# Attention scores for two heads at once: a contraction of 64 on each row half of TensorE, in place of one head with a contraction of 128

## The chip, the cores and the metric

The kernel runs on one core of a Trainium2 chip. The metric is device time of one execution in microseconds; the kernel before was run three times. One execution was recorded by the hardware profiler, and all rows below come from that recording. The engines are named as in the profile: PE is TensorE (PEld its weight loads), DVE is VectorE, ACT is ScalarE, POOL is GpSimd, SP is SyncE.

## What is computed

Two layers over 1024 latent tokens (a grid of 16 rows and 64 columns) and 256 context tokens, 1024 channels, all in float32. The first layer mixes with Fourier and Hyena channels, the second with neighbourhood attention; each ends in a SwiGLU feed-forward part. The change touches the second layer's attention alone, 16 heads of 64 channels:

```python
s_loc = jnp.einsum("bcqhd,bicjhd->bhcqij", q_r, k_b).astype(jnp.float32) * scale + bias[None]
s_loc = jnp.where(col_ok[:, :, None, :], s_loc, -jnp.inf)
s_ctx = jnp.einsum("bcqhd,bjhd->bhcqj", q_r, kc).astype(jnp.float32) * scale
s = jnp.concatenate([s_loc.reshape(B_, H, n_chunk, NA_QCOLS, n_loc), s_ctx], axis=-1)
p = jax.nn.softmax(s, axis=-1).astype(v.dtype)
```

A query sees the keys of a window around it, with a position bias, and all context keys. The softmax over both is then multiplied with the local and the context values.

## The kernel before

The kernel is written as Python code that records instructions. A scheduler then places them engine by engine, by its own estimate of when each is ready and when a buffer is free. The order in which TensorE does its work is therefore not the order of the code, and it is shown further down.

Most products are split to keep float32's accuracy: a number is written as a high and a low part, and three products are added (high by high, high by low, low by high).

Attention (`attention`, L1990) walks over eight pairs of heads. For each pair, `attn_prep` (L1895) projects keys and queries (`lin`, into the two PSUM banks of the pool `pq`) and loads and splits the values. It runs ahead of the items and is mixed in between their stages, so that its wide f16 products fill TensorE. After the last pair, the first part of the output projection (`first_part`, L2352) takes its place as filler.

The scores are made by `attn_item` (L2016). There are 64 items. Before the change an item is one head, one half of the grid's rows (`hf`) and two of the four column chunks (`c0`, `c0 + 1`), 128 queries in each chunk. A head has only 64 channels, so the code fills the array's 128 rows with the parts of the split: `kk[hd]` holds the keys' high part in the head's own 64 partitions and the low part in the other 64 (L1950 to L1959). The queries' high part must then stand in both halves, and so must the low part. Each of them is first made in its own half (L1971, L1972) and then copied to the other half by a DMA on POOL's queue (L1973 and L1974). Two products, high and low queries against the stacked keys, give all terms; they include low by low.

An item runs in three stages, and three items overlap. First it issues two loads of the bias (POOL's queue) and the scores: for the context, two chunks of 256 columns side by side in one PSUM bank, and for the local keys two banks of 384 columns (12 rows of 32). The matmuls are recorded at the helper's line, L283; 128x256 and 128x384 in f32 identify them. Then come the smallest negated score (DVE, L2041 and L2044), the exponentials (ACT, L2046 and L2048) and the transposes. For 52 of the 64 items the context part goes through a cast (ACT, L2053), a subtraction (POOL, L2054) and a transposing DMA (SP, L2055); the rest is transposed on TensorE (L2062) and split by ACT and DVE (L2065, L2066). The third stage multiplies with the values (128x65 and 128x64, f16), divides (DVE, L2088, L2089) and, after the last item of a row half, turns and stores the result (`attn_out`, L2095). During attention the PSUM tiles of all items take turns in the six banks of the pool `pp`. Before the change an item asks for three banks for scores, two or three for transposes and one for its result.

Of the kernel before, what the change touches and what calls it, by code (L numbers as in the profile page):

```python
# [19 lines left out]
P = 128  # L20
# [181 lines left out]
class Builder:  # L202
# [1692 lines left out]
    def attn_prep(self, pr, u):  # L1895
# [5 lines left out]
        kk = [self.S4(F32R), self.S4(F32R)]  # L1901
# [40 lines left out]
        for pc in (0, 1, 2):  # L1942
            for i, s in enumerate(lin(*wk, pc, acc)):
                if i == 3:
                    value(len(vt))
                if pc == 1 and i == 6:
                    wq = self.halves_of("wq", pr)
                yield s
            w = WID[pc]
            for hd in (0, 1):  # L1950
                own, other = slice(hd * 64, hd * 64 + 64), slice(64 - hd * 64, 128 - hd * 64)
                dst = kk[hd][:, pc * 512:pc * 512 + w] if pc < 2 else kc[:, hd * 256:hd * 256 + 256]
                if pc < 2:
                    nc.scalar.copy(dst[own], acc[pc][own, :w])
                    nc.vector.tensor_tensor(dst[other], acc[pc][own, :w], dst[own].bitcast(F32), SUB)
                else:
                    nc.scalar.mul(dst[own], acc[pc][own, :w], -1.0)
                    nc.vector.scalar_tensor_tensor(dst[other], acc[pc][own, :w], -1.0, dst[own].bitcast(F32),
                                                   op0=MUL, op1=SUB)  # L1959
        nxt = None  # L1960
        for pc in (0, 1):
            for i, s in enumerate(lin(*wq, pc, acc, by_chunk)):
                if i == 3:
                    value(len(vt))
                if pc == 1 and i == 3 and pr < 7:
                    nxt = self.halves_of("wk", pr + 1)
                yield s
            for hd in (0, 1):
                own, other = slice(hd * 64, hd * 64 + 64), slice(64 - hd * 64, 128 - hd * 64)
                qh, ql = self.S2(F32R), self.S2(F32R)  # L1970
                nc.scalar.mul(qh[own], acc[pc][own], self.qinv[own])  # L1971
                nc.vector.scalar_tensor_tensor(ql[own], acc[pc][own], self.qinv[own], qh[own].bitcast(F32), op0=MUL, op1=SUB)  # L1972
                for t in (qh, ql):  # L1973
                    self.ldr(t[other].bitcast(F32), t[own].bitcast(F32))  # L1974
                qs[(hd, pc)] = (qh, ql)
        self.aw = nxt
        self.prep[pr] = (qs, kk, kc, vt)
        yield 0.1

    def attn_load(self, pr):  # L1980

        qs, kk, kc, vt = self.prep[pr]
        for hf in (0, 1):
            osb = {}
            for hd in (0, 1):
                for c0 in (0, 2):
                    yield self.attn_item(pr * 2 + hd, hd, hf, c0, qs[(hd, hf)], kk[hd], kc[:, hd * 256:hd * 256 + 256], vt,
                                         osb, pr if hd == 1 and c0 == 2 else None)
# [27 lines left out]
    def attn_item(self, head, hd, hf, c0, qs, kk, kc, vt, osb, out):  # L2016

        nc, a = self.nc, self.a
        rlo = 4 * hf
        bias, loc = [], []  # L2020
        pctx = self.PS()
        for i in (0, 1):
            c = c0 + i
            b = self.G(F32, 384)
            self.ldr(b, a["bias"][head, hf, c])
# [4 lines left out]
        for i in (0, 1):  # L2030
            c = c0 + i
            q = [t[:, c * P:(c + 1) * P] for t in qs]
            ps = self.PS()
            for part in (0, 1):
                kv = kk.rearrange("p (r w) -> p r w", w=64)[:, rlo:rlo + 12, KSTART[c]:KSTART[c] + 32]
                self.mm(ps[:, :384], q[part], kv, part == 0, part == 1)
            loc.append(ps)
# [3 lines left out]
        nc.vector.tensor_reduce(cm, pctx.rearrange("p (i k) -> p i k", i=2), axis=AX, op=MIN)  # L2041
        pc = self.T()
        for i in (0, 1):
            nc.vector.tensor_tensor_reduce(bias[i], loc[i][:, :384], bias[i], -1.0, cm[:, i:i + 1], ADD, MIN,  # L2044
                                           mx[:, i:i + 1])
            nc.scalar.activation(pc[:, i * 256:i * 256 + 256], pctx[:, i * 256:i * 256 + 256], AF.Exp,  # L2046
# [3 lines left out]
        turned = 8 * (head // 2) + 4 * hf + 2 * hd + c0 // 2 < 52  # L2050
# [21 lines left out]
        for i in (0, 1):  # L2072
            c = c0 + i
            ops = []
            for g in range(3):
                gg = hf + g
                ops.append((pts[1 + i], g, c, 2 * gg + hd))
            for j in range(2):
                ops.append((pts[0], 2 * i + j, 4, 2 * j + hd))
            oo = o[:, i * 65:(i + 1) * 65]  # L2080
            for n, (t, j, cv, k) in enumerate(ops):
# [7 lines left out]
        nc.vector.tensor_tensor(osb[hf][:, c0 * P:c0 * P + 256].rearrange("p (i q) -> p i q", i=2)[:, :, hd * 64:hd * 64 + 64],  # L2089
                                both[:, :, :64], rv.unsqueeze(2).to_broadcast([P, 2, 64]), MUL)  # L2090
        if out is not None:
            self.attn_out(out, hf, osb[hf])
# [419 lines left out]
```

## Time and profile before

| | us |
|---|---|
| median of 3 runs | 2919.67 |
| lowest and highest run | 2909.61, 2922.42 |
| span of the profiled execution, first to last instruction | 2918.2 |
| attention, first scores to last values (from the span's start) | 1808 to 2230 |

The span is one execution and lies 1.5 us under the median of the runs. In a timeline row the columns are start (us from the span's start), length (us), engine, line, operation, output and inputs by tile name, shape and count. After a matmul's "128*128" (rows and columns of the array in use) stands what streams through it, partitions by columns. In a row of groups, after the count, stand busy us and mean ns of one, then the engine's idle time ahead of them and what ended it. In a row of one line, three numbers after the count are the shortest, median and longest duration in ns.

### The profile page before, as it was taken

How to read it: one execution, taken by the hardware profiler on the slowest of the kernel's cores; microseconds unless marked ns; L12 is line 12 of the kernel's file. 1: busy time of each engine (PE TensorE's matmuls, PEld its weight loads, DVE VectorE, ACT ScalarE, POOL GpSimd, SP SyncE). 2: the span in 40 equal slices, each digit the busy share in tenths (PEclk: the TensorE clock that was granted, in tenths of full speed). 3: DMA queues.
4: the chain of work that ended last, by engine and by line, in shares of the span. 5: the costliest groups of instructions: out<-in, count | busy, mean ns of one | idle time of the engine just before them, and what ended most of it. 6: DMA issues, size and time to landing. Idle time of an engine off the chain costs nothing. (4 is left out here: it accounts for less than half of the span.)

```text
span 2918.2 us, 46050 instructions
## 1 busy us (share of the span) xinstructions
PE 2766.6 (95%) x16163; PEld 1714.2 (59%) x16163; DVE 2094.0 (72%) x3833; ACT 1647.7 (56%) x2899; POOL 642.6 (22%) x1057
## 2 busy tenths in 40 slices
PE   6989999999989999999999999999999999999998
PEld 3766557888879644444555844676665444444554
DVE  4778867585467798877886767776676778775765
ACT  4674324454675667654555555676664477654553
POOL 1012013354220121213120012444443022112000
PEclk8989999999999999999999999999999999999999
DMA  6574434358785555566994798777775666424753
GB/s 254 187 265 161 161 122 151 111 168 286 285 344 182 207 205 197 201 213 240 327 333 161 273 337 294 179 188 172 185 198 188 236 226 231 153 93 184 242 191 113
DMA packets 325156, 615.98 MB, mean 211 GB/s; under 512 B 90934, under 2 KB 130552, under 8 KB 324922
## 3 DMA queue, kind: packets, MB, share of 16 engines
q1 hardware_dynamic: 252378, 384.38, 39.9%
q0 software_dynamic: 70240, 224.45, 21.6%
q10 hardware_dynamic: 2304, 4.20, 0.4%
q8 instruction: 127, 2.08, 0.3%
q14 instruction: 107, 0.88, 0.1%
HBM read 455.33 MB, written 135.53 MB: 202 GB/s over the span
## 5 line engine op out<-in xcount | busy, mean ns | idle before, releaser
L1449 PE MATMUL ps<-s,s 128*128 128x512 f16 x2592 | 582.2, 382 | 14.4 <-ACT tk L1454 6.8
L1449 PEld LDWEIGHTS <-s 128*128 128x128 f16 x2640 | 259.0, 98 | 332.6 <-issue 27.8
L283 PE MATMUL ps<-s,wh 128*128 128x256 f32 (+3 forms) x1752 | 398.2, 331 | 11.1 <-ACT wh L287 5.4
L1218 ACT ACTIVATE s<-s,c 128x512 f16<-128x512 f32 (+1 forms) x324 | 233.5, 754 | 141.9 <-DMA s<-d 79.9
L1219 DVE SCALAR_TENSOR_TENSOR s<-s,c,s 128x512 f16<-128x512 f32 (+1 forms) x324 | 247.4, 794 | 84.5 <-ACT s L1218 84.1
L1666 PE MATMUL ps<-s 128*128 128x512 f16 (+2 forms) x1308 | 303.4, 378 | 2.0 <-DVE s L1219 2.0
L283 PE MATMUL pq<-s,wh 128*128 128x512 f16 (+1 forms) x1000 | 280.3, 354 | 9.8 <-DMA wh<-d 5.4
L283 PE MATMUL ps<-s,wl 128*128 128x256 f32 (+3 forms) x876 | 261.6, 331 | 1.3 <-DVE wl L289 1.2
L283 PEld LDWEIGHTS <-wh 128*128 128x128 f16 x1664 | 160.9, 99 | 170.2 <-issue 20.9
L1666 PEld LDWEIGHTS <-s 128*128 128x128 f16 x1536 | 148.5, 98 | 178.9 <-issue 6.5
L274 POOL DMA_DIRECT2D d<-s x201 | 109.0, 543 | 640.5 <-DVE s L1510 178.6
L283 PE MATMUL ps<-s,s 128*128 128x65 f16 (+5 forms) x2666 | 222.3, 236 | 27.5 <-DMA s<-s 11.4
L335 ACT CAST mat<-cs 128x1024 fp32r<-128x1024 f16 (+2 forms) x120 | 111.6, 935 | 140.6 <-PE ps L283 57.3
L283 PEld LDWEIGHTS ps<-s,wh 128*128 128x128 f32 x1088 | 177.5, 192 | 18.1 <-ACT wh L287 5.7
L283 PE MATMUL ps<-s,mat 128*128 128x512 f32 x696 | 184.7, 413 | 3.3 <-DVE s L289 2.9
L1449 PE MATMUL ps<-s,wh 128*128 128x512 f16 x616 | 184.9, 379 | 1.8 <-DVE g L1463 1.4
L283 PE MATMUL pq<-s,wl 128*128 128x512 f16 (+1 forms) x500 | 174.5, 354 | 0.5 <-DMA wl<-d 0.5
L283 PEld LDWEIGHTS <-s 128*128 128x128 f16 x2400 | 114.5, 98 | 82.9 <-DMA s<-s 11.5
L283 PEld LDWEIGHTS ps<-s,mat 128*128 128x128 f32 x696 | 136.5, 199 | 37.9 <-DVE s L289 3.8
L1251 ACT ACTIVATE t<-s 128x1024 bf16<-128x1024 f32 (+1 forms) x164 | 141.9, 867 | 12.2 <-DVE c L470 8.4
L283 PEld LDWEIGHTS ps<-s,s 128*128 128x128 f32 (+1 forms) x746 | 113.6, 192 | 32.1 <-ACT s L287 7.0
L283 PEld LDWEIGHTS <-wl 128*128 128x128 f16 x832 | 82.3, 99 | 77.4 <-issue 4.5
(431 smaller groups left out, 5477.3 us busy)
## 6 DMA issues: line engine op xcount, KB each, us to landing
s<-d SPq DMA_DIRECT2D x294, 256.0 KB, 4.0
d<-s POOLq DMA_DIRECT2D x157, 256.0 KB, 3.2
s<-in_down SPq DMA_DIRECT2D x154, 256.0 KB, 5.4
s<-in_ada_w POOLq DMA_DIRECT2D x48, 512.0 KB, 4.8
g<-in_bias POOLq DMA_DIRECT2D x128, 192.0 KB, 3.6
s<-in_gate SPq DMA_DIRECT2D x46, 512.0 KB, 3.7
s<-in_up SPq DMA_DIRECT2D x46, 512.0 KB, 4.0
d<-g POOLq DMA_DIRECT2D x87, 256.0 KB, 2.9
```

Of the source, the lines that this page charges most:

```text
L274: self.last_ldr = self.nc.gpsimd.dma_start(out, in_).ins
L283: self.nc.tensor.matmul(o, l, r, start=st, stop=sp)
L335: self.nc.scalar.copy(m, st)
L1218: nc.scalar.activation(hi, src, AF.Copy, scale=scale)
L1219: nc.vector.scalar_tensor_tensor(lo, src, scale, hi, op0=MUL, op1=SUB)
L1251: self.nc.scalar.activation(junk[:, :t.shape[1]], t, AF.Abs, scale=2.0 ** -15, accum_out=st[:, k:k + 1])
L1449: nc.tensor.matmul(ps, x[:, sl], y, start=first and j == 0 and x is wh and y is xh, stop=j == 3 and x is wl, skip_group_check=True)
L1666: m = nc.tensor.matmul(acc[j][:, c0:c1], x[:, sl], y[:, xs], start=first and k == 0, stop=last and k == 2, skip_group_check=True)
```

## The change

An item is now one pair of heads with one column chunk; there are still 64 items with two score blocks each. The keys are kept as a high and a low tile that hold both heads, 64 partitions each (`kh`, `kl`), and so are the queries and the negated context keys. The scores of a head are three products with a contraction of 64: high by high, high by low, low by high. The code writes the two heads in turn, head 0 on partitions 0 to 63 and head 1 on 64 to 127, each into a bank of its own, so an item takes four banks for scores in place of three. The copies of the preparation work on 128 partitions at once and are half as many; the DMAs that duplicated the queries are gone. The minimum over the context scores is taken from two banks by two instructions. Transposes, values and output are the same work, indexed by head in place of chunk.

```diff
-        kk = [self.S4(F32R), self.S4(F32R)]
+        kh, kl = self.S4(F32R), self.S4(F32R)
...
-            for hd in (0, 1):
-                own, other = slice(hd * 64, hd * 64 + 64), slice(64 - hd * 64, 128 - hd * 64)
-                dst = kk[hd][:, pc * 512:pc * 512 + w] if pc < 2 else kc[:, hd * 256:hd * 256 + 256]
-                if pc < 2:
-                    nc.scalar.copy(dst[own], acc[pc][own, :w])
-                    nc.vector.tensor_tensor(dst[other], acc[pc][own, :w], dst[own].bitcast(F32), SUB)
...
+            if pc < 2:
+                self.split(acc[pc], *(t[:, pc * 512:pc * 512 + w] for t in (kh, kl)))
+            else:
+                nc.scalar.mul(kc[:, :w], acc[pc][:, :w], -1.0)
+                nc.vector.scalar_tensor_tensor(kc[:, w:], acc[pc][:, :w], -1.0, kc[:, :w].bitcast(F32),
+                                               op0=MUL, op1=SUB)
...
-            for hd in (0, 1):
-                own, other = slice(hd * 64, hd * 64 + 64), slice(64 - hd * 64, 128 - hd * 64)
-                qh, ql = self.S2(F32R), self.S2(F32R)
-                nc.scalar.mul(qh[own], acc[pc][own], self.qinv[own])
-                nc.vector.scalar_tensor_tensor(ql[own], acc[pc][own], self.qinv[own], qh[own].bitcast(F32), op0=MUL, op1=SUB)
-                for t in (qh, ql):
-                    self.ldr(t[other].bitcast(F32), t[own].bitcast(F32))
-                qs[(hd, pc)] = (qh, ql)
+            qh, ql = self.S2(F32R), self.S2(F32R)
+            nc.scalar.mul(qh, acc[pc], self.qinv)
+            nc.vector.scalar_tensor_tensor(ql, acc[pc], self.qinv, qh.bitcast(F32), op0=MUL, op1=SUB)
+            qs[pc] = (qh, ql)
...
-        pctx = self.PS()
-        for i in (0, 1):
-            c = c0 + i
...
-            q = [t[:, c * P:(c + 1) * P] for t in qs]
-            for part in (0, 1):
-                self.mm(pctx[:, i * 256:i * 256 + 256], q[part], kc, part == 0, part == 1)
...
+        pctx, loc = ([self.PS(), self.PS()] for _ in range(2))
+        qc = [t[:, c * P:(c + 1) * P] for t in qs]
+        kw = [t.rearrange("p (r w) -> p r w", w=64)[:, 4 * hf:4 * hf + 12, KSTART[c]:KSTART[c] + 32] for t in kk]
+        for acc, keys, w in ((pctx, kc, 256), (loc, kw, 384)):
+            for x, y in ((0, 0), (0, 1), (1, 0)):
+                for hd in (0, 1):
+                    r = slice(hd * 64, hd * 64 + 64)
+                    self.mm(acc[hd][:, :w], qc[x][r], keys[y][r], x == 0 and y == 0, x == 1)
...
-        nc.vector.tensor_reduce(cm, pctx.rearrange("p (i k) -> p i k", i=2), axis=AX, op=MIN)
...
+            nc.vector.tensor_reduce(cm[:, i:i + 1], pctx[i][:, :256], axis=AX, op=MIN)
```

The scheduler's order shows what becomes of this on TensorE. The first piece is one item of the kernel before, between two stretches of other work. In the first tile after MATMUL (`ps`) the product is gathered, after the arrow stand the two operands, and the size is that of the result; f32 products load their weights themselves and have no row for it:

```order
L283 MATMUL ps_20520<-s_4222_19882,s_4309_20376 128x65
L283 MATMUL ps_20569<-s_4100_19192,s_4205_19818 128x256
L283 MATMUL ps_20569<-s_4100_19192,s_4206_19819 128x256
L283 MATMUL ps_20569<-s_4100_19192,s_4205_19818 128x256
L283 MATMUL ps_20569<-s_4100_19192,s_4206_19819 128x256
L283 MATMUL ps_20578<-s_4099_19191,s_4205_19818 128x384
L283 MATMUL ps_20578<-s_4099_19191,s_4206_19819 128x384
L283 MATMUL ps_20581<-s_4099_19191,s_4205_19818 128x384
L283 MATMUL ps_20581<-s_4099_19191,s_4206_19819 128x384
L2062 MATMUL ps_20601<-c_86,g_20464 128x128 x3
```

Four context products go into one bank and two local products into each of two. The same place of the next item but one in the changed kernel, TensorE again, where the heads alternate throughout (head 0 in 20640 and 20642, head 1 in 20641 and 20643):

```order
L283 MATMUL ps_20640<-s_4102_19209,s_4211_19859 128x256
L283 MATMUL ps_20641<-s_4102_19209,s_4211_19859 128x256
L283 MATMUL ps_20640<-s_4102_19209,s_4211_19859 128x256
L283 MATMUL ps_20641<-s_4102_19209,s_4211_19859 128x256
L283 MATMUL ps_20640<-s_4102_19209,s_4212_19860 128x256
L283 MATMUL ps_20641<-s_4102_19209,s_4212_19860 128x256
L283 MATMUL ps_20642<-s_4100_19207,s_4211_19859 128x384
L283 MATMUL ps_20643<-s_4100_19207,s_4211_19859 128x384
L283 MATMUL ps_20642<-s_4101_19208,s_4211_19859 128x384
L283 MATMUL ps_20643<-s_4101_19208,s_4211_19859 128x384
L283 MATMUL ps_20642<-s_4100_19207,s_4212_19860 128x384
L283 MATMUL ps_20643<-s_4100_19207,s_4212_19860 128x384
```

Twelve products stand where eight stood, in four banks. In the item ahead of it the scheduler has written the three local products of head 0 and then those of head 1, followed by a transpose (L2082 and L2046 are the new lines of L2099 and L2062):

```order
L283 MATMUL ps_20532<-s_4100_19207,s_4211_19859 128x384
L283 MATMUL ps_20532<-s_4101_19208,s_4211_19859 128x384
L283 MATMUL ps_20532<-s_4100_19207,s_4212_19860 128x384
L283 MATMUL ps_20533<-s_4100_19207,s_4211_19859 128x384
L283 MATMUL ps_20533<-s_4101_19208,s_4211_19859 128x384
L283 MATMUL ps_20533<-s_4100_19207,s_4212_19860 128x384
L2082 MATMUL ps_20508<-c_86,s_4273_20153 128x128
```

Here only the third and fourth rows are neighbours on different row halves. In the whole order of the changed kernel the 768 score products stand in 90 unbroken stretches (512 in 94 before). Taken from the front of each stretch, 290 pairs of neighbours on different halves can be formed, and 188 products are left over. 53 of the 90 stretches are followed by transposes and the other 37 by f16 products.

More of the change, by code (lines that the diff above doesn't have):

```diff
@@ L1949, in attn_prep @@
             w = WID[pc]
-            for hd in (0, 1):
-                own, other = slice(hd * 64, hd * 64 + 64), slice(64 - hd * 64, 128 - hd * 64)
-                dst = kk[hd][:, pc * 512:pc * 512 + w] if pc < 2 else kc[:, hd * 256:hd * 256 + 256]
-                if pc < 2:
-                    nc.scalar.copy(dst[own], acc[pc][own, :w])
-                    nc.vector.tensor_tensor(dst[other], acc[pc][own, :w], dst[own].bitcast(F32), SUB)
[L1956 to L1959, printed above, removed]
+            if pc < 2:
[4 more added lines that the diff above has]
+                                               op0=MUL, op1=SUB)
         nxt = None
@@ L1984, in attn_load @@
             osb = {}
[L1985 to L1988, printed above, removed]
+            for c in range(4):
+                yield self.attn_item(pr, hf, c, qs[hf], kk, kc, vt, osb)
     def attention(self, u, fill):
@@ L2014, in attention, with attn_item @@
             pass
-    def attn_item(self, head, hd, hf, c0, qs, kk, kc, vt, osb, out):
+    def attn_item(self, pr, hf, c, qs, kk, kc, vt, osb):
         nc, a = self.nc, self.a
-        rlo = 4 * hf
-        bias, loc = [], []
-        pctx = self.PS()
-        for i in (0, 1):
-            c = c0 + i
+        bias = []
+        for hd in (0, 1):
             b = self.G(F32, 384)
-            self.ldr(b, a["bias"][head, hf, c])
+            self.ldr(b, a["bias"][pr * 2 + hd, hf, c])
             bias.append(b)
-            q = [t[:, c * P:(c + 1) * P] for t in qs]
-            for part in (0, 1):
-                self.mm(pctx[:, i * 256:i * 256 + 256], q[part], kc, part == 0, part == 1)
[L2030 to L2037, printed above, removed]
+        pctx, loc = ([self.PS(), self.PS()] for _ in range(2))
[3 more added lines that the diff above has]
+            for x, y in ((0, 0), (0, 1), (1, 0)):
+                for hd in (0, 1):
+                    r = slice(hd * 64, hd * 64 + 64)
+                    self.mm(acc[hd][:, :w], qc[x][r], keys[y][r], x == 0 and y == 0, x == 1)
         yield
@@ L2040, in attn_item @@
         cm, mx, rv = (st[:, 2 * i:2 * i + 2] for i in range(3))
-        nc.vector.tensor_reduce(cm, pctx.rearrange("p (i k) -> p i k", i=2), axis=AX, op=MIN)
         pc = self.T()
         for i in (0, 1):
+            nc.vector.tensor_reduce(cm[:, i:i + 1], pctx[i][:, :256], axis=AX, op=MIN)
             nc.vector.tensor_tensor_reduce(bias[i], loc[i][:, :384], bias[i], -1.0, cm[:, i:i + 1], ADD, MIN,
                                            mx[:, i:i + 1])
-            nc.scalar.activation(pc[:, i * 256:i * 256 + 256], pctx[:, i * 256:i * 256 + 256], AF.Exp,
+            nc.scalar.activation(pc[:, i * 256:i * 256 + 256], pctx[i][:, :256], AF.Exp,
                                  bias=mx[:, i:i + 1], scale=-1.0)
@@ L2049, in attn_item @@
         pts = [None] * 3
-        turned = 8 * (head // 2) + 4 * hf + 2 * hd + c0 // 2 < 52
+        turned = 8 * pr + 4 * hf + c < 52
         if turned:
@@ L2072, in attn_item @@
         for i in (0, 1):
-            c = c0 + i
             ops = []
@@ L2076, in attn_item @@
                 gg = hf + g
-                ops.append((pts[1 + i], g, c, 2 * gg + hd))
+                ops.append((pts[1 + i], g, c, 2 * gg + i))
             for j in range(2):
-                ops.append((pts[0], 2 * i + j, 4, 2 * j + hd))
+                ops.append((pts[0], 2 * i + j, 4, 2 * j + i))
             oo = o[:, i * 65:(i + 1) * 65]
@@ L2088, in attn_item @@
         nc.vector.reciprocal(rv, both[:, :, 64])
[L2089 to L2092, printed above, removed]
+        nc.vector.tensor_tensor(osb[hf][:, c * P:(c + 1) * P].rearrange("p (i d) -> p i d", i=2), both[:, :, :64],
+                                rv.unsqueeze(2).to_broadcast([P, 2, 64]), MUL)
+        if c == 3:
+            self.attn_out(pr, hf, osb[hf])
         yield
```

2 lines of the change are left out of this document (1 added, 1 removed).

## The prediction

> **What bounds the kernel now.** I read the page's totals first, then a table of the stretch in which attention runs, then who TensorE waited for there, then its matmuls one by one. The totals:
>
> ```profile
> span 2918.2 us, 46050 instructions
> PE 2766.6 (95%) x16163; PEld 1714.2 (59%) x16163; DVE 2094.0 (72%) x3833; ACT 1647.7 (56%) x2899; POOL 642.6 (22%) x1057
> ```
>
> The window from the first item's scores to the last item's values, first as busy time by engine (PE, PEld, DVE, ACT, POOL), with the granted clock third from the end, then as TensorE's waits (us in total, times, longest):
>
> ```profile
> 1808.00:2230.00 422.00, 400.67 (x3919) 286.09 (x3920) 296.72 (x719) 272.18 (x570) 187.36 (x314) 1.00 0.71 179
> PE ps L283 <- DMA s<-s: 11.4, 9, 3.1
> PE ps L283 <- DVE st L2044: 4.5, 8, 0.9
> PE ps L283 <- DVE s L2066: 2.3, 5, 0.7
> ```
>
> TensorE is busy for 400.67 of 422 us at the full clock, the next engine (DVE) for 297. The stage is TensorE's: what its queue loses or gains there goes into the span almost one for one, and work taken from ACT, DVE or POOL counts only through the 21 us in which TensorE waits. Of these, 11.4 us wait for DMAs from tile s to tile s, of which the transposing one (L2055) stands ahead of the values' products, and some 7 us for DVE to give back a PSUM bank.
>
> One item's scores and what stands around them, from the timeline of TensorE (start, length, count; a matmul's length includes its drain, so the step is the distance between starts):
>
> ```profile
> 1901.66 0.41 PE L2099 MATMUL ps<-c,s 128*128 128x128 f32 x2
> 1901.83 0.71 PE L283 MATMUL ps<-s,s 128*128 128x256 f32 x4
> 1902.03 0.40 PE L283 MATMUL ps<-s,s 128*128 128x256 f32 x2
> 1902.38 0.39 PE L283 MATMUL pq<-s,wh 128*128 128x512 f16 x1
> 1902.42 0.70 PE L283 MATMUL ps<-s,s 128*128 128x384 f32 x2
> 1902.97 0.39 PE L283 MATMUL pq<-s,wh 128*128 128x512 f16 x1
> 1903.19 0.38 PE L283 MATMUL pq<-s,wl 128*128 128x512 f16 x1
> ...
> 1905.29 0.82 PE L2062 MATMUL ps<-c,g 128*128 128x128 f32 x6
> 1905.94 1.62 PE L283 MATMUL ps<-s,s 128*128 128x65 f16 x34
> ```
>
> Three numbers follow. A context product (128x256) steps by (1902.38 - 1902.03) / 3 = 0.117 us. A local product (128x384) steps by 0.177: from 1902.38 to 1902.97 are 0.59 us, 0.22 of them the f16 product (its step at 1902.97 to 1903.19), and two products share the rest with a few ns over. The first context product after narrow work steps by 1902.03 - 1901.83 = 0.20, 0.083 more than its like: its weights load uncovered. Behind a 512-wide f16 product that load is covered and nothing is added. The transposes step by (1905.94 - 1905.29) / 6 = 0.108 although they stream only 128 columns: that is the time of one 128-column f32 weight load.
>
> **The change, part by part.** *Scores.* Before, an item is one head with two column chunks and takes four context and four local products; over 64 items 256 x 0.117 + 256 x 0.177 = 75.3 us. Afterwards it is two heads with one chunk and takes six and six, 768 in all instead of 512, each with 64 rows. The trace holds no half-height product, so the price lies between two ends. If nothing runs side by side, 384 x 0.117 + 384 x 0.177 = 112.9 us (+37.6). If every neighbour pair on different row halves takes the time of one product, it depends on how often they are neighbours. I counted in the order: 290 pairs stand next to each other (161 context, 129 local) and 188 products stand alone beside their own half (62 and 126), because the scheduler often writes one head's local products out before the other's. So (161 + 62) x 0.117 + (129 + 126) x 0.177 = 71.2 us: -4.1, and not the quarter that 12 / 2 against 8 suggests. Between them lies a queue of weight loads: pairs stream together, but two loads of 0.108 come one behind the other, 0.217 a pair: 161 x 0.217 + 129 x 0.217 + 62 x 0.117 + 126 x 0.177 = 92.5 us (+17.2). I take -4.1: the two products of a pair share no operand row, no weight row and no bank, and the load of one product already runs beside another's stream in the rows above (0.117 a product, where load and stream one after the other would need over 0.2). The Trainium skill (TensorE: Matmul & The Clock Gate, Part 3, Packing small matmuls) says the same, that matmuls in distinct row groups run concurrently; no run here shows it yet, and by it this term is the -4.1 taken.
>
> *Going from full height to half height and back.* The nearest rows are products with one row, elsewhere in this kernel (TensorE, then its weight loads, same columns):
>
> ```profile
> 257.82 0.63 PE L283 MATMUL ps<-s,mat 128*128 128x512 f32 x2
> 258.05 0.40 PE L283 MATMUL ps<-s,mat 128*128 128x512 f32 x1
> 258.38 0.49 PE L283 MATMUL ps<-s,s 1*128 1x512 f32 x1
> 258.72 0.39 PE L283 MATMUL ps<-s,s 1*128 1x512 f32 x1
> 259.04 0.38 PE L283 MATMUL ps<-s,s 128*128 128x256 f32 x1
> 259.26 0.40 PE L283 MATMUL ps<-s,s 128*128 128x256 f32 x2
> 258.38 0.18 PEld L283 LDWEIGHTS ps<-s,s 1*128 1x128 f32 x1 [0.37 <-issue]
> 259.04 0.30 PEld L283 LDWEIGHTS ps<-s,s 128*128 128x128 f32 x2 [0.37 <-issue]
> ```
>
> A 512-wide f32 product at full height steps by 0.23 (257.82 to 258.05). The last before the one-row product takes 0.33: 0.10 more. The load starts only then ("issue": nothing in the profile holds it) and is not covered, so the first one-row product takes 0.34, 0.11 more. Going back, 258.72 to 259.04 is 0.32, 0.09 more, and the load behind it is uncovered again (0.22 against 0.117). So a stretch of half-height products costs 0.21 to enter and 0.09 to leave. The order has 90 stretches of scores (94 before). 90 x 0.30 = 27.0 us. Before, 63 of the 94 stretches came behind narrow products or transposes and paid 0.083: 5.2 us, the others came behind wide f16 products and paid nothing. The difference is +21.8. Bounds: nothing, if 64 rows are no such case; +32, if each of the 90 also leaves with an uncovered load of 0.108. I take 21.8, from the only rows that show a change of height. The Trainium skill (TensorEngine Tiling (Array Packing), Key Properties) has a rule that speaks against this change: going from one tiling mode to another drains TensorE, going from tile to tile does not. The one-row rows agree with it, at 0.09 to 0.10 us each way; without such a drain the sum would be lower by the 21.8.
>
> *Preparation.* Each pair of heads had ten copies on ACT and ten on DVE with 64 partitions, and eight DMAs on POOL that duplicate the queries into the other half:
>
> ```profile
> L1954 ACT CAST s<-pq x32: 567/582/594, 1788.3 to 2123.0; 64x512 fp32r<-64x512 f32 x32
> L1971 ACT ACTIVATE s<-pq,c x32: 682/684/697, 1804.7 to 2161.8; 64x512 fp32r<-64x512 f32 x32
> L1958 DVE SCALAR_TENSOR_TENSOR s<-pq,s x16: 417/422/427, 1798.2 to 2131.3; 64x256 fp32r<-64x256 f32 x16
> L2041 DVE TENSOR_REDUCE st<-ps x64: 669/681/693, 1814.7 to 2214.2; 128x2 f32<-128x512 f32 x64
> L274 POOL DMA_DIRECT2D s<-s x61 | 32.1, 527 | 40.5 <-ACT s L1971 27.1 <-DVE s L1972 5.4 <-issue 4.9
> ```
>
> Half of each stays, with 128 partitions; a copy's time goes by its columns, so ACT loses 16 x 0.582 + 16 x 0.684 and eight narrower ones, some 23 us, and DVE about as much. On DVE the 64 minima of 512 columns become 128 of 256: at the 0.42 of the nearest 256-column row 128 x 0.42 - 64 x 0.68 = +10. None of this is on TensorE; it reaches the span through the 21 us of waits. POOL loses 64 issues and the 40 us it stood still ahead of them, and behind those stood the subtraction (L2054) that the transposing DMA needs, and the bias loads. At best all 11.4 us of the waits for s<-s go, at worst none. I take half, -6.
>
> *PSUM.* An item's scores hold four of the six banks instead of three (the context scores of two heads lie in two banks). TensorE's 7 us of waits for DVE to free a bank could vanish with DVE's lighter load or double; I take +4, since each item asks for 7 banks in turn where it asked for 6.
>
> Sum: -4.1 + 21.8 - 6 + 4 = +15.7. From the span of 2918.2 that is 2933.9; the median of the three runs is 1.5 above the span (2919.67), so 2935.
>
> **Rivals.** *The loads queue* (no overlap of two f32 loads): scores +17.2 in place of -4.1, and with TensorE later the waits fall by some 5 instead of 2: +17.2 + 21.8 - 5 = +34, 2954. For it: transposes and one-row products alike never load closer than 0.108 apart. Against: those all load the same rows.
>
> *The change does not do what it says*: half-height products run one behind the other. +37.6 + 21.8 - 8 = +51, 2971. For it: no row of this kernel shows two products at once. Against: nothing they share.
>
> *Not slower: no drain at 64 rows.* If a half-height product enters like any other, the second term is about 0 and the rest gives -4.1 - 6 + 4 = -6; with all 11.4 us of the DMA's waits gone and the banks no worse it is -15. So 2904 to 2914, middle 2910. It decides as soon as entering and leaving cost under 0.06 us a stretch (21.8 - 15.7 = 6 us over 90). For it: one row may be a smaller mode than 64. Against: the drain is there in every such place I looked at, both ways.
>
> **How the numbers follow.** Forecast (side by side, with drains) 44%, loads queue 24%, nothing side by side 17%, no drain 15%. The forecast's own range is 2925 to 2946 (waits and banks, each by their bounds). About 0.5%, 14.6 us, is what a measurement of this kernel can tell from no change (its three runs lie from 2909.61 to 2922.42). Below 2905 lies half of the no-drain case: faster 0.08. Up to 2934 lie its other half and under half of the forecast: same 0.27. The rest is slower, 0.65. The range runs from 2912, which leaves out two thirds of the no-drain case, to 2974, beyond the middle of the slowest: about 0.18 is left out.
>
> **What would show it.** In the changed trace the context products of two heads should start in pairs, a pair 0.117 us after the last and the second within some 0.03 us of the first; starts 0.11 apart throughout mean queued loads, starts 0.117 and 0.177 apart mean no overlap. Each stretch's first load should come 0.09 to 0.10 us late with "issue" as reason, and so should the first load behind it. The DMA row s<-s on POOL should be gone and the wait for the transposing DMA about halved; waits for L2028 (the new line of L2044) show the banks. The window of attention should grow by about 16 us, and nothing else by more than 3. The forecast is wrong if stretches enter without a late load, or if TensorE's waits move by more than 15 us.

## The result, and the profile after

The changed kernel takes 2929.6 us (median of 11 runs, 2922.70 to 2940.72) against 2914.78 of the kernel before (11 runs, 2906.14 to 2922.42): a ratio of 1.0055, 95% interval 1.0041 to 1.0069. That is 12 to 20 us slower; the prediction had 15.7. The sum was right, and so, in size, were its two terms for the products. The two for the banks and for the preparation were each too small by some 12 us in the prices measured below; they have opposite signs, so these errors cancelled, and that was luck. The clock is no part of it: the mean granted clock of the changed kernel's runs is 0.979, and so it is in the runs of the kernel before beside the experiments (0.978 to 0.979).

The totals of the changed kernel (span, then busy time by engine), and then the row of the stretch from 1808 to 2230 us:

```profile
span 2925.6 us, 46377 instructions
PE 2785.4 (95%) x16419; PEld 1707.5 (58%) x16419; DVE 2068.2 (71%) x3857; ACT 1621.2 (55%) x2859; POOL 608.7 (21%) x993
```

```profile
1808.00:2230.00 422.00, 407.01 (x4058) 271.49 (x4057) 263.45 (x730) 248.08 (x528) 154.91 (x250) 1.00 0.63 154
```

DVE, ACT and POOL are each busy for 24 to 33 us less in this stretch than before (297, 272 and 187; a little of that because the stage now reaches beyond it), and TensorE for 6 us more: work that was taken from the others did not shorten the stage. The two spans differ by 7.4 us only, the medians by 14.8. In the kernels run here the part of the program ahead of attention, the same code in all, took 1772 to 1791 us in the profiled executions, so I compare the stage itself: from the same early VectorE instruction to the last subtraction of `attn_out` it takes 448.1 us before and 462.5 after, 14.4 more. What follows the stage took 684.4 and 680.2: 4.2 less, which the prediction did not expect ("nothing else by more than 3"). In the kernels here with the query DMAs it took 682 to 684, in those without them 676 to 681.

What TensorE waited for, in us, times and longest:

```profile
PE ps L283 <- DVE st L2028: 6.8, 13, 1.8
PE ps L283 <- DVE s L2050: 4.2, 10, 0.8
PE ps L2046 <- DVE s L2072: 0.8, 2, 0.6
PE ps L2046 <- DVE s L2050: 0.8, 2, 0.6
```

The wait for the DMA s<-s (11.4) is gone; those of L283 for DVE to give back a bank, 4.5 and 2.3 before (L2044, L2066), are 6.8 and 4.2.

A stretch of half-height products, TensorE first and then its weight loads (start, length, count):

```profile
1914.51 0.27 PE L283 MATMUL pq<-s,wl 128*128 128x256 f16 x1
1914.62 0.38 PE L283 MATMUL pq<-s,wh 128*128 128x256 f16 x2
1914.93 0.80 PE L283 MATMUL ps<-s,s 64*128 64x384 f32 x6
1915.66 0.55 PE L2046 MATMUL ps<-c,g 128*128 128x128 f32 x3
```

```profile
1914.51 0.21 PEld L283 LDWEIGHTS <-wh 128*128 128x128 f16 x2
1914.93 0.48 PEld L283 LDWEIGHTS ps<-s,s 64*128 64x128 f32 x6 [0.21 <-issue]
1915.66 0.31 PEld L2046 LDWEIGHTS ps<-c,g 128*128 128x128 f32 x3 [0.25 <-issue]
```

Both halves of the forecast's mechanism are here. Six local products take 0.73 us from the first to what follows (1914.93 to 1915.66); one behind the other they would take 6 x 0.177 = 1.06. The drain is there both ways: the f16 products step by 0.11 (1914.51 to 1914.62), so the two from 1914.62 should be followed at 1914.84, and the half-height ones start at 1914.93, 0.09 late with "issue" as the reason; the next load, at full height, is late in the same way (0.25). Of the 0.73 us, 3 x 0.177 = 0.53 are stream, 0.10 the uncovered first load and 0.09 the way back. In the starts of all TensorE instructions each of the 90 stretches is entered at least 0.092 us late, most of them 0.093 to 0.094. Behind the 53 stretches that are followed by transposes the first transpose steps by 0.165 in place of 0.109 as well, 3 us in all, which the sum had only in its upper bound.

From those starts the stage can be taken apart. The first row has the score products at the steps of the prediction, in the changed kernel as if every product had a partner on the other half, with 0.083 for 63 entries before and 0.30 for 90 stretches after:

| us | before | after |
|---|---|---|
| score products and entering, leaving, if nothing held them up and all had partners | 75.3 + 5.2 = 80.5 | 56.4 + 27.0 = 83.4 |
| beyond that within score stretches | 10.9 | 24.7 |
| other products at their own steps | 330.5 | 331.6 |
| the rest: waits elsewhere, and 0.4 at the ends | 26.2 | 22.8 |
| stage | 448.1 | 462.5 |

The 56.4 is 192 x 0.117 + 192 x 0.177: every product beside one of the other head. That is not what ran. In the starts, 574 of the 768 products come in pairs, at most 20 ns apart and mostly 4: 161 pairs of context products and 126 of local ones, where the prediction counted 161 and 129. The other 194 start alone. With 0.117 or 0.177 us of stream for each, two products stream at once for 42.3 us and one by itself for 28.1, together 70.5 with rounding, and the prediction had 71.2. Twenty of the stretches hold three products of one head and nothing else, like this one between f16 products:

```profile
1911.76 0.62 PE L283 MATMUL ps<-s,s 64*128 64x256 f32 x3
1912.32 0.39 PE L283 MATMUL pq<-s,wh 128*128 128x256 f16 x2
```

The 0.56 us between the two starts are three steps of 0.117 and 0.2 for the first load and the way back. Six context products, three of each head, take no longer: 0.55 us in the stretch that starts at 1859.29. So of the 24.7 us in the second row of the table 14 are products that stream without a partner (70.5 - 56.4), and some 10.6 are waits, as many as before. The change saves 75.3 - 70.5 = 4.8 us of stream and pays 21.8 for the drains; the waits outside the stretches fall by 3.4.

### The profile page after: what moved, and what is told of

Its sections match the earlier page's. It is cut to its first block, busy times and chain, and to the rows that moved or that the text cites. A ratio compares the mean times of both kernels' runs of the same rounds, so it can differ in the third digit from the quotient of the medians.

```text
span 2925.6 us, 46377 instructions
## 1 busy us (share of the span) xinstructions
PE 2785.4 (95%) x16419; PEld 1707.5 (58%) x16419; DVE 2068.2 (71%) x3857; ACT 1621.2 (55%) x2859; POOL 608.7 (21%) x993
## 5 line engine op out<-in xcount | busy, mean ns | idle before, releaser
L1449 PE MATMUL ps<-s,s 128*128 128x512 f16 x2064 | 465.7, 380 | 10.1 <-ACT g L1454 4.2
L283 PE MATMUL ps<-s,wh 128*128 128x256 f32 (+3 forms) x1752 | 397.6, 330 | 11.7 <-ACT wh L287 5.4
L283 PE MATMUL pq<-s,wh 128*128 128x512 f16 (+1 forms) x1000 | 278.4, 353 | 6.3 <-DMA wh<-d 3.0
L283 PE MATMUL ps<-s,wl 128*128 128x256 f32 (+3 forms) x876 | 261.8, 331 | 2.5 <-DVE wl L289 1.2
L283 PEld LDWEIGHTS <-wh 128*128 128x128 f16 x1664 | 160.8, 99 | 173.1 <-issue 19.0
L283 PE MATMUL ps<-s,s 128*128 128x65 f16 (+5 forms) x2922 | 218.4, 243 | 21.1 <-DVE st L2028 6.8
L283 PE MATMUL ps<-s,mat 128*128 128x512 f32 x696 | 186.3, 415 | 3.1 <-DVE s L289 2.8
L283 PEld LDWEIGHTS ps<-s,wh 128*128 128x128 f32 x1088 | 178.3, 193 | 18.1 <-ACT wh L287 5.7
L283 PE MATMUL pq<-s,wl 128*128 128x512 f16 (+1 forms) x500 | 173.7, 353 | 0.0
L283 PEld LDWEIGHTS ps<-s,mat 128*128 128x128 f32 x696 | 137.8, 200 | 37.9 <-DVE s L289 3.2
L283 PEld LDWEIGHTS <-s 128*128 128x128 f16 x2400 | 113.9, 98 | 74.6 <-issue 14.5
L1449 PE MATMUL pq<-s,s 128*128 128x512 f16 x576 | 133.2, 380 | 1.0 <-ACT s L1218 0.6
L283 PEld LDWEIGHTS ps<-s,s 64*128 64x128 f32 (+1 forms) x1002 | 105.3, 187 | 44.7 <-issue 7.6
```

What stands on the lines that cost most here:

```text
L283: self.nc.tensor.matmul(o, l, r, start=st, stop=sp)
L1449: nc.tensor.matmul(ps, x[:, sl], y, start=first and j == 0 and x is wh and y is xh, stop=j == 3 and x is wl, skip_group_check=True)
```

## Experiments

The theory is the prediction's: products run side by side where they are neighbours on different halves, and drains cost more than the pairing saves. Its rivals are the three of the prediction; after the first runs a further one, the turnover of the PSUM banks. All ratios are to runs of the kernel before on the same chip, 95% intervals in brackets.

**Heads one behind the other.**

```diff
-            for x, y in ((0, 0), (0, 1), (1, 0)):
-                for hd in (0, 1):
+            for hd in (0, 1):
+                for x, y in ((0, 0), (0, 1), (1, 0)):
```

> The changed kernel with the loops over heads and over the three products exchanged: head 0's three products are written, then head 1's. The order then holds 168 neighbour pairs on different halves instead of 290, in 90 stretches as before. Theory (a pair of neighbours on different halves takes the time of one product, each stretch pays some 0.3 us for going to half height and back): (63 + 202) x 0.117 + (56 + 49 + 230) x 0.177 = 90.3 us of products against 71.2, so 19 us slower than the changed kernel, 35 slower than before: 1.009 to 1.015 of before. Rival one (the loss is the fourth PSUM bank) and rival two (a half-height product costs its own time whatever stands beside it): as the changed kernel, 1.0055, within 0.002.

Measured: 2916.58, 1.0019 [1.0008, 1.003]. Every theory missed. The weight loads of one item show why the first did:

```profile
1903.53 0.84 PEld L283 LDWEIGHTS ps<-s,s 64*128 64x128 f32 x12
1904.62 0.10 PEld L283 LDWEIGHTS <-wh 128*128 128x128 f16 x1 [0.26 <-issue]
```

Twelve products, three of a head at a time, need 1.09 us until the next f16 load, no more than where the heads alternate; one by one they would need 6 x 0.117 + 6 x 0.177 = 1.76. Products of two halves run together although they are three apart in the order. In this run's order 168 pairs of neighbours stand on different halves; in its trace 293 pairs start within 35 ns of each other, 182 products start alone, and the score streams take 72.4 us where the theory had 90.3. So the rule that only neighbours run together is wrong. Why this order is 10 us faster than the changed kernel was not found: the array does not explain it (72.4 us of stream against 70.5), and in the profiled stages only 4 us of it are seen (458.4 against 462.5).

**The products by themselves.** A kernel of its own issues series of 24 f32 products of 256 columns, each series between f16 products of 512 columns; it computes nothing of the reference.

> Score products by themselves, no reference work: 24 f32 products of 256 columns in each of several orders, with full-height 512-wide f16 products between them, and no waits for other engines; then 128, 384 and 512 columns, a change of height every two products, f16 halves, and quarters. Theory as revised (each half of the rows has a queue of its own): heads in turn, in blocks of four and in blocks of twelve all take about half as long as 24 full-height products (24 x 0.117 = 2.8 us): 1.4 us, and one half alone 2.8. As first forecast (only neighbours run side by side): in turn 1.4, blocks of four 2.2, blocks of twelve 2.7. A change of height, both ways, costs 0.30 us with f32 on both sides of it plus some 0.1 for a second uncovered load, and 0.30 beside f16.

TensorE's timeline: full height, the halves in turn, one half only, blocks of 4, blocks of 12:

```profile
21.41 3.22 PE L39 MATMUL b<-r 128*128 128x256 f32 x24
24.46 1.47 PE L39 MATMUL b<-h 128*128 128x512 f16 x6
25.86 1.70 PE L39 MATMUL b<-r 64*128 64x256 f32 x24
27.49 1.47 PE L39 MATMUL b<-h 128*128 128x512 f16 x6
28.89 3.13 PE L39 MATMUL b<-r 64*128 64x256 f32 x24
31.96 1.47 PE L39 MATMUL b<-h 128*128 128x512 f16 x6
33.36 1.81 PE L39 MATMUL b<-r 64*128 64x256 f32 x24
35.10 1.47 PE L39 MATMUL b<-h 128*128 128x512 f16 x6
36.50 2.75 PE L39 MATMUL b<-r 64*128 64x256 f32 x24
39.18 1.47 PE L39 MATMUL b<-h 128*128 128x512 f16 x6
```

From a row's start to the next row's: 3.05 at full height, 1.63 in turn, 3.07 on one half, 1.74 in blocks of 4, 2.68 in blocks of 12. Half height alone gains nothing; two halves together take half the time; blocks of 4 overlap almost wholly, blocks of 12 by four products only (20 steps of 0.12 instead of 12, the rest is the first load and the way out). The theory as revised held for blocks of 4 and missed for blocks of 12, where the first forecast's 2.7 came out, though not one neighbour pair but four products overlapped. Then a pair between single f16 products, in the same timeline:

```profile
62.24 0.39 PE L39 MATMUL b<-h 128*128 128x512 f16 x1
62.56 0.38 PE L39 MATMUL b<-r 64*128 64x256 f32 x2
62.87 0.39 PE L39 MATMUL b<-h 128*128 128x512 f16 x1
63.19 0.39 PE L39 MATMUL b<-r 64*128 64x256 f32 x2
```

A round takes 0.64 us in the starts of all twelve. The f16 product needs 0.216 of it and a pair 0.117; entering and leaving cost 0.307. That is the prediction's 0.30 a stretch, here measured at 64 rows. Between pairs of full-height f32 products a round takes 0.747 in the starts; less 2 x 0.120 and 0.117 that leaves 0.39, with the further 0.1 that was expected.

**The same products at full height.** Queries with zeros in the other head's rows: twelve products an item, no change of height, nothing side by side.

```diff
+            for hd in (0, 1):
+                qh, ql = self.S2(F32R), self.S2(F32R)
+                nc.scalar.mul(qh, acc[pc], self.qhalf[hd])
...
-                    self.mm(acc[hd][:, :w], qc[x][r], keys[y][r], x == 0 and y == 0, x == 1)
+                    self.mm(acc[hd][:, :w], qc[hd][x], keys[y], x == 0 and y == 0, x == 1)
```

> The changed kernel with products of full height: each head's queries get a tile with zeros in the other head's half, so the twelve products of an item run on all 128 rows and no stretch changes the height; four banks as in the change, four ACT and four DVE copies of queries per pair of heads instead of two and two. Theory: no overlap, 384 x 0.117 + 384 x 0.177 = 112.9 us, some 5.6 for loads after narrow work, no switches: 118.5 against the 108.1 that the changed kernel's scores take with entering and leaving, so 10 us slower than the changed kernel, up to 14 with the copies: 1.008 to 1.011 of before. If switching is the whole loss and pairs bring nothing: 20 us faster than the changed kernel, 0.997 to 1.000. Rival one (fourth bank): 1.0055, within 0.002.

Measured: 2951.65, 1.0137 [1.0119, 1.0154], 24 us over the changed kernel and beyond the 10 to 14 expected (23 in the profiled stages). Without drains the kernel is slower, because it loses the pairing as well: 112.9 us of stream in place of 70.5 + 27.0 are 15 us, and loads behind narrow work some 5.6 by the expectation. The run also makes 16 more copies on each of ACT and DVE, whose price here is not known. Switching alone, the second theory, forecast a faster kernel and is refuted.

**Heads kept in turn.** The order of an item's products is fixed, and the stages are recorded with the scores last.

```diff
-            for stage in range(3):
+            for nth, stage in enumerate((1, 2, 0)):
...
+                    with self.follow(last):
+                        last = nc.tensor.matmul(acc[hd][:, :w], qc[x][r], keys[y][r], start=x == 0 and y == 0,
+                                                stop=x == 1).ins
```

> The changed kernel with each score product tied in the order behind the one before it, so that the scheduler cannot take one head's products ahead, and with the stages recorded in the order transposes, values, scores. The order then holds 374 neighbour pairs (191 context, 183 local) in 84 stretches. Theory: (191 + 2) x 0.117 + (183 + 18) x 0.177 = 58.2 us of products against 71.2 and six switches fewer: 15 us faster than the changed kernel, about before: 0.997 to 1.003. Rival one (fourth bank) and rival two: 1.0055, within 0.002.

Measured: 3033.93, 1.041 [1.0389, 1.0431]. It missed, and it says nothing of pairing: the recorded order puts the transposes (L2049 here) right behind the exponentials (L2035) that they need. Its granted clock is lower too: 0.960 to 0.966 in its four runs, 0.976 to 0.982 in those of the changed kernel.

```profile
PE ps L2049 <- ACT g L2035: 62.3, 44, 2.7
```

**Four banks in the kernel before.** The context chunks in two banks, two minima; all else as before.

```diff
-        pctx = self.PS()
+        pctx = [self.PS(), self.PS()]
...
-                self.mm(pctx[:, i * 256:i * 256 + 256], q[part], kc, part == 0, part == 1)
+                self.mm(pctx[i][:, :256], q[part], kc, part == 0, part == 1)
```

> The kernel before with the two context chunks of an item in two PSUM banks instead of one, and the minimum over them in two instructions as in the change; nothing else. The order has 119 stretches of full-height scores instead of 94. Theory (the fourth bank costs a few us at most): 1.000 to 1.002 of before. Rival one (the fourth bank is the loss): 1.004 to 1.006.

Measured: 2929.78, 1.006 [1.0038, 1.0083]: 11 to 24 us for a bank, where the prediction had 4. TensorE's waits, with the old line numbers:

```profile
PE ps L283 <- DVE st L2044: 8.5, 7, 2.4
PE ps L2062 <- DVE st L2044: 7.4, 10, 1.5
```

Its 4.5 us of waits for L2044 become 16, while the wait for the DMA s<-s falls from 11.4 to 1.6: the ratio is what both leave. The order changed with it: the 94 stretches of scores are 119.

**Three banks in the changed kernel.** The context scores of two column chunks share a bank per head and are made in the even item, with one minimum for both.

```diff
+        if not odd:
+            two["ctx"] = [self.PS(), self.PS()]
...
+        jobs = [(c, loc, kw, 384)]
+        if not odd:
+            jobs = [(c + j, [t[:, j * 256:j * 256 + 256] for t in ctx], kc, 256) for j in (0, 1)] + jobs
```

> The changed kernel with the context scores of two column chunks made together, the two chunks of one head side by side in one bank: an even item takes four banks, an odd one two, three on average as before the change; the minimum is again taken over 512 columns at once. Same products, same halves. Theory (the fourth bank is what the change pays beside the switches; the kernel before with four banks was 1.006): 10 to 17 us faster than the changed kernel, 0.998 to 1.002 of before. If the banks are not it: 1.0055, within 0.002.

Measured: 2916.50, 1.0012 [1.0003, 1.0021]: the bank's price, seen from the other side, is some 12.5 us (1.0055 to 1.0012). That includes the order it brings, with 83 stretches in place of 90 (2 us of drains); the profiled stages show 5.7 of it (456.8 against 462.5). One way in which the fourth bank costs TensorE time is to be seen in the changed kernel, here one item (TensorE, then DVE):

```profile
1926.88 1.16 PE L283 MATMUL ps<-s,s 64*128 64x256 f32 x9
1928.46 0.76 PE L283 MATMUL ps<-s,s 64*128 64x384 f32 x3 [0.42 <-DVE s L2050]
1929.15 0.33 PE L2082 MATMUL ps<-c,s 128*128 128x128 f32 x1
```

```profile
1927.76 0.56 DVE L2050 TENSOR_TENSOR s<-ps,s 128x384 f16<-128x384 f32 x1 [0.96 <-ACT s L2049]
1928.23 0.28 DVE L2072 TENSOR_TENSOR s<-ps,st 128x128 f32<-128x128 f32 x1
```

Nine of the twelve products run. The last three, one head's local ones, have no bank until DVE has split the transposes of an earlier item (1927.76 to 1928.32). They wait 0.42 us and then run alone, with no partner left, as the other head's three did before them: this item takes 1.19 us more than its 1.18. Of the 44 items whose twelve products stand unbroken, 13 took 0.9 us or more too long; all 44 together 17.1 us. The list of waits shows only the part in which the whole engine stands still. A half without a partner counts as busy.

**No query DMAs.** In the kernel before, ACT and DVE write all 128 partitions of the queries and the 64 DMAs are gone; as many copies as before, and the other half holds the other head's queries.

```diff
-                nc.scalar.mul(qh[own], acc[pc][own], self.qinv[own])
-                nc.vector.scalar_tensor_tensor(ql[own], acc[pc][own], self.qinv[own], qh[own].bitcast(F32), op0=MUL, op1=SUB)
-                for t in (qh, ql):
-                    self.ldr(t[other].bitcast(F32), t[own].bitcast(F32))
+                nc.scalar.mul(qh, acc[pc], self.qinv)
+                nc.vector.scalar_tensor_tensor(ql, acc[pc], self.qinv, qh.bitcast(F32), op0=MUL, op1=SUB)
```

> The kernel before without its 64 DMAs that duplicate the queries: the ACT and DVE copies write all 128 partitions, so the other half of each query tile holds the other head's queries instead of the duplicate (the scores are then other numbers, of the same sizes). Nothing else changes. Theory: POOL's queue is free for the subtraction ahead of the transposing DMA, and TensorE's waits fall by 3 to 8 us: 0.997 to 0.999 of before. Rival (the DMAs were hidden): 1.000, within 0.001.

Measured: 2896.10, 0.9939 [0.9927, 0.9951]. The sign was right; the size, 14 to 21 us, is far beyond the 3 to 9 us expected. TensorE's wait for transposing DMAs and DVE's for the bias, which were 11.4 and 28.3:

```profile
PE ps L283 <- DMA s<-s: 2.4, 3, 1.0
...
DVE g L2042 <- DMA g<-in_bias: 12.9, 14, 2.6
```

**The same DMAs on SyncE's queue**, in the kernel before:

```diff
-                    self.ldr(t[other].bitcast(F32), t[own].bitcast(F32))
+                    self.ld(t[other].bitcast(F32), t[own].bitcast(F32))
```

> The kernel before, with the 64 query DMAs issued from SyncE's queue in place of POOL's. If their cost is POOL's queue (the 40 us that it stood still ahead of them, with bias loads and subtractions behind), 0.992 to 0.998. Rival, if the cost is the transfers' own traffic and landing time: 0.999 to 1.002; if they now hold up the transposing DMAs behind them, 1.003 or more.

Measured: 2909.48, 0.9974 [0.9961, 0.9987]. As expected if it is POOL's queue, though less than half of what taking the DMAs away gave. The profiled execution, the longest of its twelve, has no shorter stage (450.1 against 448.1), so where the 6 us were gained is not seen. The bias comes sooner (DVE's wait was 28.3 before), the transposing DMAs hardly:

```profile
DVE g L2044 <- DMA g<-in_bias: 12.6, 16, 3.0
...
PE ps L283 <- DMA s<-s: 8.8, 7, 2.7
```

**The duplicates by ACT and DVE**, in the kernel before:

```diff
+                for to in (own, other):
+                    nc.scalar.mul(qh[to], acc[pc][own], self.qinv[own])
+                    nc.vector.scalar_tensor_tensor(ql[to], acc[pc][own], self.qinv[own], qh[to].bitcast(F32), op0=MUL, op1=SUB)
```

> The kernel before, with the 64 DMAs that duplicate the queries replaced by ACT and DVE writing the other half themselves (four copies more on each per pair and chunk, 32 x 0.684 + 32 x 0.745 us in all); the same numbers as before. If what those DMAs cost is their place in POOL's queue ahead of the bias loads, the gain of the run without them (0.9939) stays: 0.992 to 0.997. Rival, if that gain came from the halved copies on ACT and DVE: 0.998 to 1.004.

Measured: 2925.34, 1.0037 [1.002, 1.0053]. The number falls to the rival, but not its reason as it was written: the kernel without DMAs had halved nothing, it has the 32 copies of the kernel before on each engine. Between those two kernels lie 32 more copies on ACT and 32 on DVE, 22 and 24 us of busy time on engines that had over 100 us to spare, and 29 us of time. The projections' banks are held longer, and TensorE waits for that, though its 5.3 us are a small part of the 29, whose cause is not shown in full:

```profile
PE pq L283 <- DVE s L1973: 5.3, 9, 2.0
...
ACT s L1972 <- DVE s L1973: 27.8, 27, 3.3
```

**Two products in place of three.** The changed kernel without high queries by low keys: 18.8 us less for TensorE to stream if all run in pairs.

```diff
-            for x, y in ((0, 0), (0, 1), (1, 0)):
+            for x, y in ((0, 0), (1, 0)):
```

> The changed kernel without the products of high queries and low keys: two products a head instead of three (this leaves out part of the scores' accuracy), everything else as in the change. TensorE has 64 x (0.117 + 0.177) = 18.8 us less of score stream. Theory (TensorE's own work still sets the stage): 10 to 19 us faster than the changed kernel, 0.999 to 1.002 of before. Rival (with four banks an item the stage goes by the turnover of the banks, whatever TensorE has to do): within 5 us of the changed kernel, 1.004 to 1.006.

Measured: 2942.42, 1.0099 [1.0083, 1.0116], 13 us over the changed kernel with a third of its score products gone. Both theories missed. TensorE's and DVE's waits, and the row of the stage with its neighbourhood:

```profile
PE ps L283 <- DVE st L2028: 17.2, 18, 3.1
PE ps L2046 <- DVE s L2072: 6.0, 6, 2.4
...
DVE g L2028 <- DMA g<-in_bias: 39.1, 23, 4.3
1790.00:2270.00 480.00, 444.28 (x4051) 281.14 (x4048) 281.96 (x767) 262.00 (x549) 156.95 (x257) 0.96 0.61 152
```

What TensorE no longer does turns into waits, and the granted clock is lower. It is 0.96 in this row (0.99 in the changed kernel's), with 41 us of the stage at half clock (3.4 us there), and 0.973 in each of this kernel's four runs, against a mean of 0.979. An estimate from these shares: 0.006 of 2940 us are 18 us, more than the 13 that the kernel is slower. So this run does not show that the return of the banks sets the stage whatever TensorE has to do; how the time divides between waits and clock, and why the clock fell, is open. DVE's wait for the bias made the bias buffers a suspect (four, so two items' worth; each is freed by an item's transposes, after which POOL loads the next).

**Bias blocks in the pool of 34 tiles**, in the changed kernel:

```diff
-            b = self.G(F32, 384)
+            b = self.S2(F32, 384)
```

> The changed kernel, with the bias blocks in the pool of 34 half-size tiles in place of their own pool of four. If the items wait on the return of a bias buffer (transposes free it, then POOL loads the next, then DVE can work and free the score banks), DVE's 24.5 us of waits for the bias shrink to under 10 and the ratio falls to 0.996 to 1.002. Rival, if the four banks alone hold the items back: DVE's waits change little and the ratio stays at 1.004 to 1.007.

Measured: 2929.10, 1.0039 [1.0021, 1.0057], between the two expectations and not told apart from the changed kernel (1.0041 to 1.0069). The bias wait went as the theory asked, the time did not follow:

```profile
DVE s L2028 <- DMA s<-in_bias: 6.9, 8, 1.9
...
PE ps L283 <- DVE st L2028: 11.8, 10, 2.5
```

So the bias buffers were not what held TensorE up; its wait for score banks is longer here than in the changed kernel (6.8), though the profiled execution is the longest of the eight (2937.2).

**Three banks and one head behind the other**, the two edits that had gained, with the diffs shown at each:

> The changed kernel with two chunks' context scores in one bank and the heads' products written one head after the other: the two edits that gained 0.0043 and 0.0036 apart. If they act on different waits they add up: 0.995 to 0.999, a little faster than the kernel before. Rival, if both only reshuffle the scheduler's order: 1.000 to 1.006.

Measured: 2914.04, 0.9999 [0.9985, 1.0014]. The interval touches both expectations. It is 0.0056 below the changed kernel, where the two gains would add up to 0.0079 and the larger alone is 0.0043. The intervals do not tell it from three banks alone (1.0003 to 1.0021), so whether the gains add up is open; it is level with the kernel before.

## Why the prediction was right, and where it was not

*Switching height*, +21.8: right. 0.093 to 0.094 us to enter, 0.307 us a stretch in all by the products alone, where one-row products had given 0.30; transposes behind a stretch add 3 us. The no-drain rival is refuted. The Trainium skill (TensorEngine Tiling (Array Packing), Key Properties) has this drain, and the rows agree with it.

*Side by side*, -4.1: right in size, -4.8 in the trace, with 287 pairs where 290 were counted. The rule behind the count was wrong: not only neighbours in the order pair up. A half can take its next product ahead of earlier ones for the other half; by themselves, products of one half overtook up to three of the other, and with the heads one behind the other 293 pairs ran where the rule gave 168. In the changed kernel the rule's count came out even so, because many of the products it left over have none of the other head within reach: stretches that hold one head alone, stretches of nine that end with three of one head, and items whose second bank comes late. That the counts agree so closely is partly luck. The rivals with queued loads and with nothing side by side are refuted by the pairs' starts, mostly 4 ns apart; the loads start in pairs too, 6 to 9 ns apart in the stretch of six shown above.

*Banks*, +4: too small. One more bank costs 11 to 24 us in the kernel before, and giving it back gains some 12.5 in the changed one, both with the order that comes with it. "Each item asks for 7 banks in turn where it asked for 6" was the right thing to look at, but I priced it from the 7 us of waits there were. That was no bound: the price measured is larger than the wait.

*Preparation*, -6: too small as well. In the kernel before the 64 DMAs alone are worth 14 to 21 us. I had bounded them by TensorE's direct wait for s<-s, 11.4; behind them in POOL's queue stood also the bias loads, for which DVE waited. Moving the DMAs off that queue gave less than half, so the rest of their price is open. How much the halved copies brought to the changed kernel was not tried by itself; 32 copies on each of ACT and DVE more cost 29 us in the kernel before.

With these measured the sum is -4.8 + 21.8 - 18 + 17 = +16, and +14.8 was measured. The last two come from kernels with the old products, each with a range of 7 to 13 us, and need not add up in the changed one. Its trace shows only what they leave together: waits of 10.6 + 22.8 us in place of 10.9 + 26.2, -3.7 where -6 + 4 = -2 was taken. Each edit makes the scheduler write another order (78 to 119 stretches of scores in these kernels). The changed kernel and the one with the heads one behind the other do the same work with the same banks and lie 10 us apart (1.0055, 1.0019), so the luck of an order may be worth as much as these terms. No run holds the order fixed and changes one price, and the one that fixed it by hand fixed a bad one.

## What to carry to other kernels

In these runs a product with half the contraction costs as much as one with all of it, unless a product on the other half stands within about four places in the order; together the two take the time of one. A stretch of them costs 0.3 us to enter and leave, and one pair saves 0.117 to 0.177, so stretches should be long, and both halves should be in them: here a quarter of the products found no partner. In a stage that turns over few PSUM banks, count the banks an item takes as well as TensorE's microseconds: one bank an item was worth more than the saving in products. A small wait for a buffer is no upper bound for what one more buffer taken will cost. And when an edit that takes work away makes a kernel slower, look at the granted clock as well as at the waits.

## What the runs showed of the hardware

Products on different row halves do not keep the order of the program. The trace does not name the half, but in the blocks of 12 the starts form two series some 0.12 apart: the first product of the second block starts 7 ns after the ninth of the first, 0.11 us ahead of the tenth, so it overtook three. The Trainium skill (TensorE: Matmul & The Clock Gate, Part 3, Packing small matmuls) has products start and end in strict order; this run shows otherwise for the starts of f32 products on two halves. The same section's 4 ns from one packed product to the next agrees with the 1 to 10 ns here where the halves take turns. Four quarters run at once, too: 24 products of 32 rows and 256 columns take 0.91 us (77.59 to 78.50), and f16 products pair like f32 ones, 24 of 512 columns on the two halves in 2.70 us from the first start to the next f16 product (70.68 to 73.37). The quarters, and what follows them:

```profile
77.59 0.98 PE L39 MATMUL b<-r 32*128 32x256 f32 x24
78.50 1.47 PE L39 MATMUL b<-h 128*128 128x512 f16 x6
```

The granted clock differs with the kernel: 0.976 to 0.982 in the runs of the changed kernel, 0.973 in every run with two products in place of three, 0.960 to 0.966 in every run with the heads kept in turn. In the profile of the run with two products it was 0.5 in ten short spells of the stage, 41 us in all.
